# Two edits to a planned two-layer encoder kernel: output transposes due later, and the order of four low-rank products

## The chip, the cores and the metric

The kernel runs on one core of a Trainium2 chip, as one program. The metric is the device time of an execution in microseconds (us). A core has five engines with queues of their own: TensorE (PE in the rows; PEld is its weight loads), VectorE (DVE), ScalarE (ACT), GpSimd (POOL) and SyncE (SP, which only issues DMAs here).

## What is computed

Two layers. Each normalises its input, projects it once, sends the columns of the projection through four head groups, and maps the four gated outputs back.

```python
for l in range(DEPTH):                       # 2 layers, 1024 tokens, width 1024
    h = rms_norm(x, norm_pre[l])
    p = h @ w_in[l]                          # one projection, columns split among A, B, C, D
    y_a = head_layer_norm(mlstm(...) * sigmoid(a_o)) * silu(a_z)           # A: chunks of a matrix memory
    decay_logit = rwkv_w0[l] + jnp.tanh(w_lo) @ rwkv_w_up[l]               # B: low-rank up-projection 1
    a_b = sigmoid(rwkv_a0[l] + a_lo @ rwkv_a_up[l])                        # B: low-rank up-projection 2
    y_b = (head_layer_norm(rwkv7_scan(...)) + gn_b + bonus) * silu(b_z)    # B: delta rule
    y_c = rglru(...) * silu(c_z)                                           # C: gated linear recurrence
    y_d = head_layer_norm(retention(...)) * silu(d_z)                      # D: retention
    y = concat([y_a, y_b, y_c, y_d]) @ w_out[l]
    x = x + rms_norm(y, norm_post[l])
```

## The kernel before, in words

**Units.** Each head group is cut into four units of two heads (A0 to D3). A unit has projection pieces (products of the normalised input with weight columns, in PSUM banks of tag `pj`, three of them), and a mixer, a Python generator that handles the 1024 tokens in four quarters of 256. The mixers of A, D and C work in the two PSUM banks of tag `mx`, those of B in the three banks of tag `bc`.

**Order.** Nobody waits for anything while the program is written out: a planner (`Clock`, `Driver`) keeps a model of each engine's time and decides from it which step is written next into the queues. `Driver.run` (line 535) looks at five threads of mixer steps. A step may be written when its own time has come (the modelled end of its last step plus `SLACK`, 1.0 us) and two banks of its tag are free by the model. When no thread can go, a stretch of a projection piece is written instead: projections fill the gaps. On the chip TensorE takes its matmuls in the order so written, and waits where an operand or a bank is late.

**Output transposes.** A quarter of a mixer of A, D or B ends with a layer norm over each head (`ln_groups`, line 575: VectorE reductions, a square on ScalarE, a power on GpSimd, and as last step a VectorE multiply `t<-t,sm` or `bl<-bl,smB`). Its result has to be transposed. That is not written at once: `drv.later` (line 525) notes a closure, with the due time `clock.step + LATE`, where `clock.step` is the modelled end of the step that holds the norm. `Driver.run` writes the closure once it is due and one bank of its tag (`mx` for A and D, `bc` for B) is free by the model:

```python
self.flush(*[kind for kind, (t, _) in self.ends.items() if t <= now and clock.banks("bc" if kind == "B" else "mx", 1) <= now])
```

The next norm of the same kind writes it in any case (`drv.flush`, lines 1035, 1199, 1300). The closure is `out_a` (line 1207, for A and D) or `end` (line 1042, for B): a PSUM bank, two 128x128 transposes on TensorE, one ScalarE read of the bank, for B one VectorE add, and a store to DRAM by SP. There are 64 of `out_a` (4 quarters, 8 units, 2 layers) and 32 of `end`.

**Low-rank up-projections.** `prep` (line 812), a stage of B that runs 32 times, computes the two up-projections into two banks `wps` and `aps`. The weights are split in a high and a low part (`lu[0]`, `lu[1]`); for each bank there is one full product (128 rows: high weights times both parts of the input) and one half-row product (64 rows: low weights times the high part), the two accumulating in the bank. The half-row products of the two banks use rows 0 to 63 and rows 64 to 127. Behind them stand the two products of `head_sums` with a matrix of ones (`psbc<-cc,onesr` in the rows).

All instructions are recorded through one wrapper, so every row carries line 256; tiles tell them apart: `psmx<-ident,t` are the transposes of `out_a`, `psbc<-ident,bl` those of `end`, `psbc<-lora,luh` the full low-rank products, `psbc<-lora,lul` the half-row ones.

Of the kernel before, what the change touches and what calls it, by code (L numbers as in the profile page):

```python
# [132 lines left out]
TM = 2  # L133
NAT = [3,5,7,9]
CH = 6
SLACK, LATE = 1.0, 2.5
STEP = "step"
QA = 256
QB = 256
# [123 lines left out]
def trunk(ctx: ExitStack, tc, x, wch, wa, wd, wg, wo, pv, gb, lup, lrw, npost, cst, dtab, out):  # L263
    nc = tc.nc
    clock = Clock()
    V, A, Pl, PE, DQ = (Timed(e, n, clock) for e, n in ((nc.vector, "DVE"), (nc.scalar, "ACT"), (nc.gpsimd, "POOL"), (nc.tensor, "PE"),
                                                        (nc.sync, "SP")))
# [8 lines left out]
    def T(tag, shape, dt=F32):  # L276
        uid[0] += 1
        t = sb.tile(list(shape), dt, tag=tag, bufs=BUFS[tag], name=f"{tag}_{uid[0]}")
        if tag != "pr":
            clock.place(tag, clock.key(t), BUFS[tag])  # L280
        return t
# [16 lines left out]
    def PT(tag):  # L298
        uid[0] += 1
        t = psum.tile([128, 512], F32, tag=tag, bufs=PSB[tag], name=f"ps{tag}_{uid[0]}")  # L300
        clock.place("ps" + tag, clock.key(t), PSB[tag])
        return t
# [474 lines left out]
    def unit_b(l, P, hTs, j, drv):  # L777
# [34 lines left out]
        def prep(qt):  # L812
# [5 lines left out]
            lu = st["lu"]  # L818
# [6 lines left out]
            lo_ = T("lora", (128, 2, QB), F32R)  # L825
# [7 lines left out]
            wps = PT("bc")  # L833
            aps = PT("bc")
            for n, p in enumerate((wps, aps)):
                hp = slice(64 * n, 64 * n + 64)
                PE.matmul(p[:, 0:QB], lu[0][:, n, :], lo_[:, n, :], start=True, stop=False)
                PE.matmul(p[:, 0:QB], lu[1][hp], lo_[hp, n, :], start=False, stop=True)
            nps = PT("bc")
            head_sums(nps, kparts)  # L840
# [213 lines left out]
        def preps():  # L1054
            yield lambda: st["p"] == 6 and P.lora_done

            raw = bt((128, 2, 128))
            for n in range(2):
                for part in range(2):
                    DQ.dma_start(raw[64 * part:64 * part + 64, n, :], lup[l, 64 * n:64 * n + 64, j * 128:(j + 1) * 128])  # L1060
            lu = (T("luh", (128, 2, 128), F32R), T("lul", (128, 128), F32R))
            A.copy(lu[0], raw)
            for n in range(2):
                hp = slice(64 * n, 64 * n + 64)
                V.tensor_tensor(lu[1][hp], raw[hp, n, :], lu[0][hp, n, :].bitcast(F32), ALU.subtract)
            st["lu"] = lu
            for qt in range(S // QB):
                yield from prep(qt)
# [512 lines left out]
```

## Time and profile before

| | |
|---|---|
| median of 3 runs | 2573.94 us (2569.77 to 2581.92) |
| the profiled execution, its own time | 2583.34 us |
| span of the profiled execution, first to last instruction | 2581.6 us |
| TensorE matmuls, busy | 2407.5 us (93%), 16032 instructions |
| VectorE busy | 1788.8 us (69%) |
| ScalarE busy | 1036.4 us (40%) |
| GpSimd busy | 407.4 us (16%) |
| mean granted TensorE clock | 0.978 of full |

A row of the timeline gives the start, the time from the first start to the last end of the instructions it merges, the engine, the operation, out<-in by the program's names, shapes, and how many (x2). Brackets at its end give the idle time of the engine just before it and what ended that. Ends of matmuls are modelled, so the distance between two starts tells more about TensorE than a duration. A wait is charged to what came last: a transpose that waits "for DVE t" may wait for the norm's result or for a PSUM bank that a VectorE instruction was reading.

### The profile page before, as it was taken

Reading aid. Unit: us, or ns where it says so; the run is one execution under the profiler, and the core shown is the slowest. Engines: PE = TensorE matmul, PEld = TensorE weight load, DVE = VectorE, ACT = ScalarE, POOL = GpSimd, SP = SyncE. Lnnn points to the kernel's source line nnn. Section 1 sums busy time; section 2 is a strip of 40 time slices with the busy share of each in tenths; the row PEclk is TensorE's granted clock in tenths of the full one; section 3 lists DMA queues with packets and bytes.
Section 4 is the critical chain, followed back from the end, with each engine's and each line's share of the span. In section 5 each row is a group of like instructions: output and inputs, shape, how many; then the busy total and the mean of one; then the engine's idle time right before and its main releaser. Section 6 shows DMA issues by size and latency. Waiting matters only on the chain. (4 is left out here: it accounts for less than half of the span.)

```text
span 2581.6 us, 45006 instructions
## 1 busy us (share of the span) xinstructions
PE 2407.5 (93%) x16032; PEld 1977.6 (77%) x16032; DVE 1788.8 (69%) x5526; ACT 1036.4 (40%) x2261; POOL 407.4 (16%) x536
## 2 busy tenths in 40 slices
PE   7999999999999999999999989999999999999998
PEld 5787887787787777777777878877877877777776
DVE  5668877878767767455476678778787777763464
ACT  5323434534533543233354234336344335533333
POOL 2202212112111110001122111211121111100010
PEclk9999999999999999999999999999999999999999
DMA  5322232222323233275533222322223222333764
GB/s 157 106 61 75 63 88 81 72 74 77 89 74 79 67 106 102 86 245 186 187 121 104 59 74 69 88 79 64 73 82 90 68 77 81 95 98 118 249 205 150
DMA packets 219237, 265.82 MB, mean 103 GB/s; under 512 B 72708, under 2 KB 122244, under 8 KB 219012
## 3 DMA queue, kind: packets, MB, share of 16 engines
q1 hardware_dynamic: 210308, 254.54, 32.9%
q0 software_dynamic: 8704, 8.39, 1.4%
q8 instruction: 127, 2.08, 0.3%
q14 instruction: 98, 0.80, 0.1%
HBM read 201.76 MB, written 61.08 MB: 102 GB/s over the span
## 5 line engine op out<-in xcount | busy, mean ns | idle before, releaser
L256 PE MATMUL pspj<-hT,hi 128*128 128x512 f32 x2880 | 950.0, 409 | 3.6 <-ACT hT L256 2.7
L256 PEld LDWEIGHTS pspj<-hT,hi 128*128 128x128 f32 x2880 | 524.9, 192 | 107.8 <-ACT hT L256 3.2
L256 PE MATMUL pspj<-hT,lo 128*128 128x512 f32 x1440 | 573.6, 398 | 0.0
L256 PE MATMUL pspj<-hi,hT 128*128 128x256 f32 x2048 | 418.0, 294 | 0.3 <-ACT hi L256 0.3
L256 ACT CAST hi<-raw 128x512 fp32r<-128x512 f32 x372 | 229.7, 618 | 384.3 <-PE pspj L256 214.8
L256 PEld LDWEIGHTS pspj<-hi,hT 128*128 128x128 f32 x2048 | 337.8, 196 | 6.7 <-issue 1.3
L256 PEld LDWEIGHTS pspj<-hT,lo 128*128 128x128 f32 x1440 | 275.0, 191 | 59.4 <-DVE lo L256 0.4
L256 DVE TENSOR_TENSOR lo<-raw,hi 128x512 fp32r<-128x512 f32 x306 | 216.1, 707 | 146.5 <-ACT hi L256 142.8
L256 PE MATMUL pspj<-lo,hT 128*128 128x256 f32 x1024 | 294.9, 288 | 4.6 <-DVE lo L256 4.6
L256 PEld LDWEIGHTS pspj<-lo,hT 128*128 128x128 f32 x1024 | 200.6, 196 | 5.8 <-DVE lo L256 5.3
L256 DVE SCALAR_TENSOR_TENSOR NT<-PA,NT 128x20 f32<-128x20 f32 (+15 forms) x768 | 147.3, 243 | 68.7 <-DMA PA<-pd 64.4
L256 POOL TENSOR_TENSOR lo<-raw,hi 128x512 fp32r<-128x512 f32 x66 | 87.1, 1320 | 554.4 <-ACT hi L256 476.9
L256 POOL TENSOR_TENSOR sm<-sm,mhalf 128x4 f32<-128x4 f32 (+1 forms) x96 | 88.1, 918 | 455.0 <-DVE sm L256 361.1
L256 ACT ACTIVATE t<-t 128x256 f32<-128x256 f32 (+1 forms) x132 | 54.4, 412 | 215.0 <-DVE t L256 200.8
L256 PE MATMUL pspj<-hi,pr 128*128 128x512 f32 x384 | 132.6, 399 | 1.1 <-DVE c L256 1.1
L256 PE MATMUL psbc<-hi,pr 128*128 128x512 f32 x384 | 131.1, 395 | 0.0
L256 DVE SCALAR_TENSOR_TENSOR pr<-c,pv,pr 128x512 f32<-128x512 f32 x144 | 109.0, 757 | 10.7 <-ACT pr L256 9.7
L256 PE MATMUL psmx<-pr,t 128*128 128x65 f32 (+3 forms) x768 | 112.5, 282 | 1.9 <-DVE t L256 1.9
L256 POOL TENSOR_TENSOR cc<-bt,cc 128x256 fp32r<-128x256 f32 x64 | 51.2, 807 | 343.3 <-ACT cc L256 340.8
L256 PEld LDWEIGHTS psmx<-pr,t 128*128 128x128 f32 x768 | 101.8, 198 | 3.9 <-DVE t L256 2.6
L256 DVE TENSOR_TENSOR NT<-NT,inv 128x24 f32<-128x24 f32 (+13 forms) x480 | 94.9, 198 | 8.1
L256 DVE TENSOR_SCALAR bS<-psbc,wc 64x64 f32<-64x64 f32 x256 | 74.3, 290 | 37.3 <-PE psbc L256 31.1
(274 smaller groups left out, 4064.4 us busy)
## 6 DMA issues: line engine op xcount, KB each, us to landing
raw<-in_wch_dram SPq DMA_DIRECT2D x180, 256.0 KB
raw<-in_wo_dram SPq DMA_DIRECT2D x128, 256.0 KB
PA<-pd SPq DMA_DIRECT2D x64, 256.0 KB
zmix<-c SPq DMA_DIRECT2D x64, 256.0 KB
rkv<-ymix SPq DMA_DIRECT2D x64, 256.0 KB
rkv<-c SPq DMA_DIRECT2D x48, 256.0 KB
rkv<-rkv SPq DMA_DIRECT2D x32, 384.0 KB
lora<-lora POOLq DMA_DIRECT2D x32, 256.0 KB, 3.5
```

The costliest lines, as they stand in the source:

```text
L256: res = fn(*args, **kw)
```

## The change

`LATE` goes from 2.5 to 6.0 us: the transposes of a norm become due 3.5 us of modelled time later. In `prep` the two full products come first, then the two half-row ones. The planner sees both, and may write everything behind them in another order. No instruction is added or taken away.

```diff
@@ -133,7 +133,7 @@
-SLACK, LATE = 1.0, 2.5
+SLACK, LATE = 1.0, 6.0
@@ -833,8 +833,9 @@
             for n, p in enumerate((wps, aps)):
+                PE.matmul(p[:, 0:QB], lu[0][:, n, :], lo_[:, n, :], start=True, stop=False)
+            for n, p in enumerate((wps, aps)):
                 hp = slice(64 * n, 64 * n + 64)
-                PE.matmul(p[:, 0:QB], lu[0][:, n, :], lo_[:, n, :], start=True, stop=False)
                 PE.matmul(p[:, 0:QB], lu[1][hp], lo_[hp, n, :], start=False, stop=True)
```

## Rows read from the trace of the kernel before

**Rows 1.** The page, part 1: busy time of each engine, share, instructions.
```profile
PE 2407.5 (93%) x16032; PEld 1977.6 (77%) x16032; DVE 1788.8 (69%) x5526; ACT 1036.4 (40%) x2261; POOL 407.4 (16%) x536
```

**Rows 2.** Waits of PE: who, for whom, us in total, times, longest.
```profile
PE psmx L256 <- DVE t L256: 49.3, 36, 3.5
```

**Rows 3.** Groups of PE: busy us, mean ns | idle us before, releasers.
```profile
L256 PE MATMUL psmx<-ident,t 128*128 128x128 f32 x128 | 26.8, 292 | 38.6 <-DVE t L256 35.9 <-DVE inv L256 2.4
...
L256 PE MATMUL psbc<-ident,bl 128*128 128x128 f32 x64 | 12.8, 282 | 3.7 <-DVE NT L256 1.2 <-DVE bl L256 1.0 <-ACT bt L256 1.0
```

**Rows 4.** Timeline of PE: transposes that waited, and steps behind two of them.
```profile
216.04 0.44 PE L256 MATMUL psmx<-ident,t 128*128 128x128 f32 x2 [1.15 <-DVE t L256]
...
385.54 0.44 PE L256 MATMUL psmx<-ident,t 128*128 128x128 f32 x2 [2.63 <-DVE t L256]
...
389.12 0.58 PE L256 MATMUL psmx<-aS,t 128*128 128x130 f32 x1
...
593.61 0.44 PE L256 MATMUL psmx<-ident,t 128*128 128x128 f32 x2 [2.33 <-DVE t L256]
...
594.97 0.65 PE L256 MATMUL psmx<-aS,t 128*128 128x130 f32 x2 [0.22 <-issue]
...
806.15 0.44 PE L256 MATMUL psmx<-ident,t 128*128 128x128 f32 x2 [3.45 <-DVE t L256]
```

**Rows 5.** Timeline of DVE around three of these waits.
```profile
215.55 0.43 DVE L256 TENSOR_TENSOR t<-t,sm 128x256 f32<-128x256 f32 x1 [0.82 <-POOL sm L256]
...
380.88 0.42 DVE L256 TENSOR_TENSOR t<-t,sm 128x256 f32<-128x256 f32 x1 [0.35 <-POOL sm L256]
...
385.06 0.42 DVE L256 SCALAR_TENSOR_TENSOR t<-psmx,t 128x256 f32<-128x256 f32 x1
...
385.47 0.42 DVE L256 SCALAR_TENSOR_TENSOR t<-psmx,t 128x256 f32<-128x256 f32 x1
...
594.44 0.42 DVE L256 TENSOR_TENSOR t<-pr,t 128x256 f32<-128x256 f32 x1
```

**Rows 6.** Windows at half clock behind eight waits: busy us, PEclk, DMA, GB/s.
```profile
386.89:390.30 3.41, 3.41 (x29) 2.96 (x27) 2.62 (x9) 1.62 (x4) 1.46 (x2) 0.50 0.39 118
...
806.73:816.97 10.24, 10.20 (x42) 7.85 (x41) 5.94 (x17) 3.54 (x10) 0.00 (x0) 0.50 0.13 27
...
sum 47.80, PE 47.71 PEld 38.52 DVE 28.27 ACT 16.99 POOL 3.17; mean PE 5.96 PEld 4.81 DVE 3.53 ACT 2.12 POOL 0.40
```

**Rows 7.** Timeline of PE: one of the 32 low-rank groups, and its neighbours.
```profile
204.31 0.28 PE L256 MATMUL pspj<-hi,hT 128*128 128x256 f32 x1
204.43 0.28 PE L256 MATMUL psbc<-lora,luh 128*128 128x256 f32 x1
204.64 0.38 PE L256 MATMUL psbc<-lora,lul 64*128 64x256 f32 x1
204.95 0.38 PE L256 MATMUL psbc<-lora,luh 128*128 128x256 f32 x1
205.27 0.38 PE L256 MATMUL psbc<-lora,lul 64*128 64x256 f32 x1
205.58 0.50 PE L256 MATMUL psbc<-cc,onesr 128*128 128x256 f32 x2
```

**Rows 8.** Timeline of PE: half-row products that alternate between the two row halves.
```profile
225.22 0.38 PE L256 MATMUL psbc<-ident,KB 128*128 128x128 f32 x2
225.53 1.16 PE L256 MATMUL psbc<-AR,KB 64*128 64x128 f32 x16
226.62 0.38 PE L256 MATMUL psmx<-aS,t 128*128 128x130 f32 x1
```

**Rows 9.** Timeline of PE: last transposes of B in layer 1, first output product.
```profile
1095.02 0.38 PE L256 MATMUL psbc<-ident,bl 128*128 128x128 f32 x2
...
1103.43 0.39 PE L256 MATMUL psmx<-hi,pr 128*128 128x512 f32 x1
```

**Rows 10.** Waits of SP's queue: stores of transposed outputs among them.
```profile
SPq L256 <- ACT t L256: 139.5, 35, 11.9
```

## The prediction

> **What bounds the kernel.** I read the engines' busy shares first. TensorE is busy for 2407.5 of 2581.6 us and the next engine, VectorE, for 69% [rows 1]: the end is set by TensorE's queue, so what counts is its idle time (174 us), its pace, and its switches. The second view is who TensorE waited for: the largest entry is 49.3 us in `mx` banks for VectorE's `t` [rows 2]. Grouped by instruction, most of it stands in front of the output transposes of A and D: 38.6 us, and 3.7 us in front of B's [rows 3]. The timeline shows 25 waits of over 0.4 us there (38.3 us, 1.53 us each), 13 in the first layer and 12 in the second; the other 39 pairs hardly wait.
>
> What they wait for is the point. Some wait for the norm: at 216.04 the pair starts as the norm's multiply ends (215.55 + 0.43) [rows 4, 5]. These are about 9.6 us. The rest (about 29 us) wait for a bank. At 385.54 the norm's multiply had ended at 381.30, but VectorE's read of a score bank ended at 385.48, and that is when the pair started [rows 4, 5]: the planner held the bank for free and the chip was later than the model. The third view is the granted clock: behind eight of these waits it fell to half (0.50, the 1.2 GHz level) for 47.8 us in all; TensorE was busy in 47.71 of them [rows 6]. At half the pace that is up to 23.9 us of lost work.
>
> **Part 1, the later due time.** Nothing is added; what moves is, 64 times, two transposes, a ScalarE read and an SP store, and 32 times the same with a VectorE add. Ends of the gain: nothing, and 38.6 + 3.7 + 23.9 = 66.2 us.
>
> The norm kind should vanish: no transpose of that kind is later than its place by more than 1.97 us, and the move is 3.5. For the bank kind the question is what is late next. I walked behind each of the 25 waits to the next step whose operand was fresh. Three classes:
> - Free: the pair at 385.54 waited 2.63 us. The next step of that chain is at 389.12, and its last score operand was ready at 385.89 [rows 4, 5]. Moved up by 2.63 it would start at 386.5 and not wait. Six waits are like this, 11.1 us; I count 10.
> - Taken over: the pair at 593.61 waited 2.33 us, but the recurrence step at 594.97 starts 0.1 us after its own operand (594.44 + 0.42) [rows 4, 5]. Without the transposes TensorE comes to that step earlier and waits there. Nine waits, 12.2 us; I count nothing, and leave their half clock too.
> - Between: ten waits, 14.9 us, the two longest (3.45 us at 806.15 [rows 4], and its twin in the second layer) among them; another transpose wants the next `mx` bank behind them. I count a third, 5 us.
>
> So 15 of 38.3 us. The clock by the same classes: of the 47.8 us at half, 6.8 lie behind free waits (386.89 to 390.30 is one), 17.1 behind taken-over ones, 23.9 behind those between (10.24 at 806.73, its twin the same, 3.4 elsewhere) [rows 6]. Half of a stretch is lost work: 3.4 us come back in the first class and half of 12 in the third: 9.4 us. B's 3.7 us I leave.
>
> What the move can cost: the pairs now come among the recurrence steps, which take `mx` banks too, and a bank that the model calls free can be held there as well. No row shows those places. The nearest row is the present place [rows 3]: 25 of 64 waiting, 1.53 us each. The ends are none waiting (nothing) and all 64 (98 us). I take four, 6 us, nearer to none, because the 39 pairs that do not wait already arrive later behind their norm than the waiting ones. The store moves with its transposes: SP waited 139.5 us for ScalarE's `t` [rows 10], with loads behind; a store that is written later lets the loads written meanwhile pass. I count that as nothing: no wait of TensorE in the mixers is ended by a DMA or by SP. B's transposes are the last of the layer's mixers at 1095.02, and the projections fill TensorE until 1103.43 [rows 9]: 8.4 us cover a later B; beyond that each us costs one. After the last step of all, the closure is written at once in either kernel.
>
> Part 1: 15 + 9.4 - 6 = 18 us gained.
>
> **Part 2, the four products.** Starts before: full 204.43, half-row 204.64, full 204.95, half-row 205.27, ones 205.58 [rows 7]: 1.15 us from the first to the next work. A 256-column product behind one of the same shape takes 0.12 us (204.31 to 204.43), so nearly all the rest is switching: 0.21 us into half rows from a streaming full product, 0.31 us from half to full rows, and 0.32 again. After: full to full 0.12, full to half 0.21, half to half, half to ones 0.31. The two half-row products lie in different row halves and banks. Of such a mix there is a row: sixteen products of 128 columns in alternating halves take 226.62 - 225.53 - 0.31 = 0.78 us, 0.052 each, while full-row ones of 128 columns are 0.11 apart (0.38 less the 0.27 of one) [rows 8]. So two go in the time of one, and the second adds about 0.01 here. Sum: 0.65 us, a gain of 0.50 us, times 32 = 15.9 us. Ends: if the pair does not run side by side (0.12) and the entry costs 0.31, it is 0.86 us and a gain of 0.29 us, 9.3 us in all. I take 0.50, the row of the same mix of halves. TensorE stands at no operand there, so it is on the path; but where the next wait hangs on older work of another engine it is eaten. Some 170 waits in 2582 us are one per 15 us; with operand chains of some 3 us that is one group in five: 12.7 us.
>
> Read by durations the result would be another: the half-row product is shown with 0.38 us and the full one with 0.28 [rows 7]. The Trainium skill, Perfetto Trace Analysis, section on per-instruction lifecycle, says that a matmul's end is estimated from its size and not observed; the starts here agree, being 0.12 us apart under bars of 0.28. By durations alone the edit would bring nothing, since all four bars stay. The Trainium skill, TensorEngine Tiling (Array Packing), Key Properties, says that changing the tiling mode drains the array and that tiles of one mode run in parallel; the rows of the switches and of the alternating halves agree, and by that rule alone the whole 0.50 us holds.
>
> **Sum.** 18 + 13 = 31 us, 1.2%. From the profiled execution: 2583 - 31 = 2552. That one is 9.4 us above the median of the three, so the median goes to 2574 - 31 = 2543.
>
> **Rivals.**
> - Carried over: every wait moves to the next step of the chain, or the due time does not decide because the bank condition does. For: nine waits are of that kind already. Against: six are not. Part 1 is then 0 - 6, part 2 gives 13: 2567, within half a per cent. Chance 0.22.
> - All of it: no wait is left and the clock stays up: 66 + 16 = 82 us, 2492; between it and the forecast lie the times around 2510. For: 3.5 us exceeds all 25 waits. Against: the taken-over class. Chance 0.12.
> - Slower: the transposes collide with the recurrence in the two `mx` banks. Place: the pair between two state steps, whose bank VectorE empties late. Price: 1.53 us a wait plus 0.95 us of clock (23.9 / 38.6 of it), 2.48 us. It uses up part 2 when 5 more pairs wait than now (30 of 64), and makes the kernel slower by over half a per cent from 35. With all 64: 97 us lost against 13, 2658. For: rows at 385 and 806 show the model early by up to 3.5 us. Against: the late readers there stood behind DMAs that have landed by the new place. Chance 0.14.
> - My forecast, part of the waits and most of part 2: 0.52, with a range of its own of 2522 to 2560.
>
> **How the numbers follow.** Half a per cent, 13 us, is about what a measurement of this kernel can tell from no change. Faster by more: nearly all of the forecast (0.50), the all-of-it case (0.12), a fifth of the carried-over one (0.05): 0.67. Slower by more: most of the collision case, 0.12. Same: 0.21. The range runs from 2508, half-way into the all-of-it case, to 2582, past the carried-over one and the start of the collision.
>
> **What would show it.** Right: idle before `psmx<-ident,t` falls from 38.6 to some 10 us; idle before `psmx<-aS,t` and `psmx<-pr,t` grows by less than 15; the stretch at half clock near 806 gets shorter or goes; the starts from the first `luh` to `onesr` are 0.65 us apart, the two `lul` within 0.02. Wrong: idle in front of the transposes stays and its releaser is `aS` or `dS`; or the recurrence steps wait for ScalarE's `t<-psmx`; or a gap opens between B's last transposes and the output product; or the planner, whose whole order shifts with both edits, puts new waits in places that no row here shows.

## The result, and the profile after

The changed kernel takes 2596.7 us (median of 4 runs, 2590.1 to 2598.6) against 2574.5 of the kernel before in the same job: a ratio of 1.0075, 95% interval 1.0046 to 1.0103. It is 22 us slower by the medians (19 by the ratio); the forecast was 31 us faster. The profiled execution has a span of 2593.9 us, 12.3 above that of before, and it is this pair that the rows below compare.

First what the edits were meant to do. The page's first part, against [rows 1]:

```profile
PE 2385.5 (92%) x16032; PEld 1973.8 (76%) x16032; DVE 1779.6 (69%) x5526; ACT 1030.5 (40%) x2261; POOL 414.3 (16%) x536
```

TensorE is busy for 22 us less with the same instructions; the low-rank groups below account for 15.4 of them. Groups of TensorE (busy us, mean ns, idle us before and its releasers), first after:

```profile
L256 PE MATMUL psmx<-hi,pr 128*128 128x512 f32 x256 | 93.0, 405 | 16.8 <-ACT pr L256 16.1 <-ACT hi L256 0.8
...
L256 PE MATMUL psmx<-pr,pr 64*128 64x128 f32 x256 | 37.3, 317 | 32.4 <-DVE t L256 24.6 <-ACT pr L256 6.0 <-DVE inv L256 1.4
L256 PE MATMUL psmx<-ident,t 128*128 128x128 f32 x128 | 26.3, 288 | 10.9 <-DVE t L256 6.4 <-ACT cc L256 4.6
L256 PE MATMUL psmx<-aS,t 128*128 128x130 f32 x112 | 24.4, 300 | 13.5 <-issue 11.4 <-DVE t L256 1.3 <-DVE aS L256 0.9
...
L256 PE MATMUL psbc<-ident,bl 128*128 128x128 f32 x64 | 12.9, 284 | 13.9 <-DVE bl L256 13.9
```

and three of the same groups before (the other two are in [rows 3]):

```profile
L256 PE MATMUL psmx<-hi,pr 128*128 128x512 f32 x256 | 91.4, 397 | 3.0 <-ACT pr L256 2.0 <-ACT hi L256 0.9
...
L256 PE MATMUL psmx<-pr,pr 64*128 64x128 f32 x256 | 33.3, 303 | 12.5 <-DVE t L256 7.9 <-DVE NT L256 3.1 <-DVE inv L256 1.4
...
L256 PE MATMUL psmx<-aS,t 128*128 128x130 f32 x112 | 25.9, 315 | 2.7 <-issue 1.8 <-DVE aS L256 0.8
```

Idle time in front of the output transposes fell from 38.6 us [rows 3] to 10.9, as forecast. Part of it came back: 32.4 us in front of `psmx<-pr,pr` (12.5 before) and 13.5 in front of `psmx<-aS,t` (2.7 before), 31 us more in two groups; and 16.8 us stand in front of the output products (`psmx<-hi,pr`, 3.0 before) and 13.9 in front of B's transposes (3.7 before). By release, TensorE's waits in `mx` banks for `t` went from 49.3 [rows 2] to 35.5 us; `psmx` for ScalarE's `pr` and `psbc` for `bl` are the new ones:

```profile
PE psmx L256 <- DVE t L256: 35.5, 30, 3.3
PE psbc L256 <- DVE bS L256: 25.1, 26, 2.1
PE psmx L256 <- ACT pr L256: 23.3, 7, 7.2
PE psbc L256 <- DVE TQ L256: 16.8, 12, 3.0
PE psbc L256 <- DVE bl L256: 13.9, 4, 5.4
```

SP's queue, with the later stores in it, hardly changed (139.5 us in [rows 10]):

```profile
SPq L256 <- ACT t L256: 145.9, 41, 17.9
```

The low-rank group does what was forecast. Timeline of TensorE (start, us, ..., idle before in brackets):

```profile
1480.07 0.40 PE L256 MATMUL psbc<-lora,luh 128*128 128x256 f32 x2
1480.39 0.38 PE L256 MATMUL psbc<-lora,lul 64*128 64x256 f32 x2
1480.70 0.50 PE L256 MATMUL psbc<-cc,onesr 128*128 128x256 f32 x2
```

From the first `luh` to `onesr` 0.63 us, where 0.65 were forecast and 1.15 were read before [rows 7]; the two half-row products end 0.38 us after the first of them starts, which is the length of one. Summed over the 32 groups this distance fell from 41.2 to 25.8 us, by 15.4.

TensorE thus has less to do, and the projections of a layer end earlier: the last one of layer 1 ends at 1087.96, in the kernel before at 1103.6. Its waits only moved: from a layer's first low-rank product to its last projection TensorE stands idle for 65.8 and 70.2 us in the two layers, against 63.4 and 65.6 before. And the layer does not end earlier. Timeline of TensorE at the end of layer 1, against [rows 9]:

```profile
1093.40 0.58 PE L256 MATMUL psbc<-bS,TQ 128*128 128x128 f32 x2 [0.70 <-DVE bS L256]
1099.37 0.66 PE L256 MATMUL psbc<-ident,bl 128*128 128x128 f32 x2 [5.38 <-DVE bl L256]
1106.82 0.80 PE L256 MATMUL psmx<-hi,pr 128*128 128x512 f32 x1 [6.78 <-ACT pr L256]
```

and of layer 2:

```profile
2386.05 0.66 PE L256 MATMUL psbc<-ident,bl 128*128 128x128 f32 x2 [5.39 <-DVE bl L256]
2393.96 0.79 PE L256 MATMUL psmx<-hi,pr 128*128 128x512 f32 x1 [7.25 <-ACT pr L256]
```

B's last transposes moved from 1095.02 to 1099.37 in layer 1 (in layer 2 from 2374.36 to 2386.05), and nothing is left to lie over them: TensorE waits 5.4 us for B's last norm, then 6.8 us until the stored result has been loaded again, together with its gate, and made an operand. Windows of 10 us there (busy us of PE, PEld, DVE, ACT, POOL, then the granted clock):

```profile
1080.00:1090.00 10.00, 9.78 (x108) 7.30 (x107) 2.75 (x7) 4.13 (x10) 1.68 (x3) 1.00 0.16 54
1090.00:1100.00 10.00, 2.54 (x10) 1.34 (x10) 4.60 (x17) 1.14 (x3) 1.01 (x1) 0.68 0.18 53
1100.00:1110.00 10.00, 3.22 (x9) 2.47 (x9) 3.19 (x5) 1.80 (x3) 0.00 (x0) 0.50 0.73 225
```

In the kernel before the same three windows are full:

```profile
1080.00:1090.00 10.00, 10.00 (x48) 8.28 (x47) 4.83 (x12) 2.85 (x7) 0.00 (x0) 1.00 0.31 107
1090.00:1100.00 10.00, 10.00 (x46) 8.25 (x45) 4.05 (x8) 2.80 (x6) 1.36 (x1) 1.00 0.46 146
1100.00:1110.00 10.00, 10.00 (x44) 7.91 (x43) 5.70 (x10) 4.01 (x7) 1.28 (x1) 1.00 0.88 290
```

In all, from a layer's first low-rank product to its first output product, layer 1 grew by 2.6 us (1012.8 to 1015.4) and layer 2 by 9.5 (1014.6 to 1024.1): 12.1 of the 12.3 us.

So a layer has two limits: TensorE's queue with its filler (the projections that are written into the gaps), which got shorter, and B's sixteen quarters, which got longer. **B's chain** is read below as the time from the start of the layer's first `psbc<-lora,luh` to the start of its last `psbc<-ident,bl`: 1004.4 and 1005.9 us before, 1008.0 and 1016.2 after. Two quarters of B are in flight; the first stage of a quarter is written only when the mixer of the quarter two before it is done (`drv.mixed`).

### The profile page after: what moved, and what is told of

Same layout as the page of the kernel before. It is cut to its first block, busy times and chain, and to the rows that moved or that the text cites. A ratio compares the mean times of both kernels' runs of the same rounds, so it can differ in the third digit from the quotient of the medians.

```text
span 2593.9 us, 45063 instructions
## 1 busy us (share of the span) xinstructions
PE 2385.5 (92%) x16032; PEld 1973.8 (76%) x16032; DVE 1779.6 (69%) x5526; ACT 1030.5 (40%) x2261; POOL 414.3 (16%) x536
## 5 line engine op out<-in xcount | busy, mean ns | idle before, releaser
L256 PE MATMUL pspj<-hT,hi 128*128 128x512 f32 x2880 | 946.7, 408 | 2.7 <-ACT hT L256 2.3
L256 PEld LDWEIGHTS pspj<-hT,hi 128*128 128x128 f32 x2880 | 525.8, 192 | 109.1 <-issue 3.6
L256 PE MATMUL pspj<-hT,lo 128*128 128x512 f32 x1440 | 574.2, 399 | 0.0
L256 PE MATMUL pspj<-hi,hT 128*128 128x256 f32 x2048 | 417.9, 294 | 0.8 <-ACT hi L256 0.8
L256 ACT CAST hi<-raw 128x512 fp32r<-128x512 f32 x372 | 229.5, 619 | 387.4 <-PE pspj L256 205.5
L256 PEld LDWEIGHTS pspj<-hi,hT 128*128 128x128 f32 x2048 | 339.3, 197 | 5.9 <-ACT hi L256 1.2
L256 PEld LDWEIGHTS pspj<-hT,lo 128*128 128x128 f32 x1440 | 275.5, 191 | 60.4
L256 DVE TENSOR_TENSOR lo<-raw,hi 128x512 fp32r<-128x512 f32 x306 | 212.9, 699 | 154.2 <-ACT hi L256 152.7
L256 PE MATMUL pspj<-lo,hT 128*128 128x256 f32 x1024 | 296.1, 289 | 3.7 <-DVE lo L256 3.7
L256 DVE SCALAR_TENSOR_TENSOR NT<-PA,NT 128x16 f32<-128x16 f32 (+15 forms) x768 | 150.4, 246 | 89.8 <-DMA PA<-pd 85.2
L256 PEld LDWEIGHTS pspj<-lo,hT 128*128 128x128 f32 x1024 | 201.7, 197 | 4.6 <-DVE lo L256 4.1
L256 POOL TENSOR_TENSOR lo<-raw,hi 128x512 fp32r<-128x512 f32 x66 | 90.7, 1376 | 629.4 <-ACT hi L256 505.1
L256 POOL TENSOR_TENSOR sm<-sm,mhalf 128x4 f32<-128x4 f32 (+1 forms) x96 | 90.4, 941 | 447.1 <-DVE sm L256 411.8
L256 PE MATMUL pspj<-hi,pr 128*128 128x512 f32 x384 | 132.7, 399 | 0.0
L256 PE MATMUL psbc<-hi,pr 128*128 128x512 f32 x384 | 130.9, 394 | 0.0
L256 ACT ACTIVATE t<-t 128x256 f32<-128x256 f32 (+1 forms) x132 | 54.1, 411 | 187.2 <-DVE t L256 176.7
L256 DVE SCALAR_TENSOR_TENSOR pr<-c,pv,pr 128x512 f32<-128x512 f32 x144 | 108.5, 753 | 7.0 <-ACT pr L256 6.3
L256 PE MATMUL psmx<-pr,t 128*128 128x65 f32 (+3 forms) x768 | 108.4, 277 | 0.3 <-DVE t L256 0.3
L256 PE MATMUL psmx<-hi,pr 128*128 128x512 f32 x256 | 93.0, 405 | 16.8 <-ACT pr L256 16.1
L256 POOL TENSOR_TENSOR cc<-bt,cc 128x256 fp32r<-128x256 f32 x64 | 52.6, 829 | 347.9 <-ACT cc L256 326.1
L256 DVE TENSOR_TENSOR NT<-NT,inv 128x24 f32<-128x24 f32 (+13 forms) x480 | 95.9, 200 | 8.7
L256 PEld LDWEIGHTS psmx<-pr,t 128*128 128x128 f32 x768 | 97.6, 193 | 2.3 <-DVE t L256 0.8
```

The lines of the kernel that those rows point to most:

```text
L256: res = fn(*args, **kw)
```

## The experiments

Eighteen kernels beside the two; each ratio is to the runs of the kernel before in the same job, with its 95% interval. "Plan" is what the planner's own model gives for the place of B's last quarter, in us from the start of layer 1; the last two columns are B's chain as defined above, each from one profiled execution. Executions of the same kernel differ (2570.8 to 2592.1 us for the kernel before in one job), so differences of a few us in these columns mean little.

```
run                     median   ratio (interval)          plan  B's chain, layer 1, 2
before                  2574-79  1                         1012  1004.4  1005.9
after                   2596.7   1.0075 (1.0046-1.0103)    1039  1008.0  1016.2
e1_late_only            2605.6   1.0112 (1.0083-1.0141)    1039  1013.9  1011.8
e2_order_only           2597.5   1.0087 (1.0060-1.0113)    1014  1004.4  1016.0
e3_late_a_only          2607.7   1.0124 (1.0099-1.0149)    1036  1021.0  1014.8
e4_late_b_only          2605.9   1.0104 (1.0075-1.0133)    1029  1015.1  1017.7
e5_after_held           2595.2   1.0066 (1.0042-1.0091)    1017  1015.7  1009.9
e6_late_held            2547.0   0.9881 (0.9860-0.9902)     997   981.9   986.4
e7_order_held           2595.4   1.0074 (1.0044-1.0103)    1016  1010.3  1005.9
e8_after_more_filler    2604.4   1.0106 (1.0069-1.0142)       -  1018.9  1004.4
e9_before_lean          2572.9   0.9982 (0.9963-1.0001)    1010   997.2   998.1
e10_before_late_1_5     2596.8   1.0068 (1.0048-1.0088)    1043  1009.9  1014.9
e11_order_late_5        2547.8   0.9880 (0.9859-0.9902)    1001   985.7   981.2
e12_both_held_late_5    2576.2   0.9980 (0.9960-1.0000)     999  1003.2   996.5
e13_old_list_products   2569.1   0.9964 (0.9946-0.9981)       -   995.8  1001.9
e14_old_list_both       2572.1   0.9966 (0.9949-0.9984)       -   997.2   993.9
e15_new_list_undone     2614.5   1.0142 (1.0114-1.0169)       -  1017.1  1031.5
e16_late5_list_undone   2577.0   0.9999 (0.9982-1.0017)       -   996.0   990.8
e17_new_list_c_moved    2606.2   1.0101 (1.0077-1.0125)       -  1016.0  1024.0
e18_old_list_c_moved    2580.0   1.0000 (0.9985-1.0015)       -  1001.3  1004.3
```

### Which edit is it? e1 to e4

e1 has `LATE` 6.0 with the old order of the products, e2 the new order with `LATE` 2.5. e3 and e4 have both edits, with `LATE` 6.0 for one kind of transposes alone:

```diff
-            self.ends[kind] = clock.step + LATE, fn
+            self.ends[kind] = clock.step + (LATE if kind == "A" else 2.5), fn     # e3; e4: "B"
```

> The due time alone (6.0 us; the four products in the old order). Cover theory: what sets a layer's end is B's chain of quarters, and projections are only filler; a shorter filler moves no end once B's last transposes and the 7.5 us from there to the first output product are bare. The late due time then makes B's last transposes later and is the edit that costs: 8 to 22 us slower than before, a gap of 5 us or more in front of the first output product in each layer. Collision theory: the loss is new waits of TensorE inside the mixers; 10 to 30 us slower with no gap at the layer's end.

> The four products alone (due time 2.5 us as before). Both theories: starts of the group 0.65 us apart instead of 1.15, so 8 us less filler a layer. Cover theory: the first output product can begin at the earliest 7.5 us behind B's last transposes, it began 8.4 us behind, so at most 1 us a layer comes out, plus or minus what the planner's new order moves B's last transposes: within 6 us of before. TensorE theory (all that TensorE is spared comes out): 12 to 16 us faster.

> Both edits, but the due time of 6.0 us only for A's and D's transposes; B's are due after 2.5 us as before. If B's own late transposes lengthen B's chain, this one has B's last transposes where they were and is within 6 us of before, or faster by up to 4. If A's and D's late transposes delay B (they hold nothing of B's, but shift the planner's order), it is as slow as the changed kernel, 10 to 22 us.

> Both edits, but the due time of 6.0 us only for B's transposes. If B's own late transposes lengthen the chain: 10 us or more slower, as the changed kernel. If it is A's and D's: within 6 us of before.

The expectations do not decide it: e1 is 29 us slower, with TensorE bare at the layer's end, where the cover theory had at most 22; e2 fits neither theory; e3 and e4, meant to tell the two kinds of transposes apart, are both as slow as the changed kernel or slower (1.0124 and 1.0104). Each edit alone is slower, by 1.1 and 0.9%, and both together are no slower than one. That effects don't add up like this speaks against costs of the edits themselves; what all five kernels share is that the planner wrote a new order. e13 to e16 test it.

### A stay in B's chain, and a hold against it: e5 to e7

In the changed kernel quarter 5 of B (counted from 0) stands in layer 1 for 24.5 us between the start of its last inverse products and its first product with the state; in before no quarter stays over 6.1 us there. Timeline of TensorE, after:

```profile
474.93 0.67 PE L256 MATMUL psbc<-G,AP 64*64 64x128 f32 x16
...
495.86 0.40 PE L256 MATMUL psmx<-TQ,lrl 128*128 128x512 f32 x1
...
499.39 0.49 PE L256 MATMUL psbc<-bS,TQ 128*128 128x128 f32 x2 [1.77 <-DVE TQ L256]
```

VectorE ran the inversion of the other quarter from 466.8 to 487. The hold lets an inversion be written only while B's other quarter is not between these two steps:

```diff
-            yield lambda: st["ready"] >= qt
+            yield lambda: st["ready"] >= qt and not drv.tq     # set ahead of the TQ step, cleared behind it
```

e5 is the changed kernel with the hold, e6 is e1 with it, e7 is e2 with it.

> The changed kernel, but an inversion is not written while B's mixer stands between its AP products and the VectorE step that makes TQ. Collision with the inversion (new theory): in the changed kernel the planner writes the inversion of one quarter of B (a run of small VectorE steps some 20 us long) just ahead of the TQ step of the other, so the first state product follows the G,AP products after 24.5 and 16.3 us in two quarters of layer 1, where before it was never over 6.1. Held back, no quarter is over 9 us, the first output product comes 15 us or more a layer earlier, and the kernel is 14 to 36 us faster than the changed one: 2560 to 2583. Mixer-waits theory (bank waits of TensorE in the mixers cost the time): the hold touches no mx bank, so within 6 us of the changed kernel, 2590 to 2603.

> The late due time alone with the same hold. New theory: its two or three long gaps a layer (27.3, 23.9 and 14.5 us in layer 1) go, 57 us of gaps a layer, and with them 20 us or more: 2560 to 2585, and under that of the late due time alone (2605) in any case. Mixer-waits theory: 2598 to 2612.

> The new order of the products alone with the same hold. New theory: its gaps of 9.2 and 10.8 us go, some 20 us a layer; B's last transposes then come 5 to 10 us earlier in layer 2, and the kernel is within 8 us of before, or faster: 2564 to 2586. If gaps of 10 us have nothing to do with it, it stays at 2597.

In e5 the longest stay is 12.9 us, and the time is that of the changed kernel: the stay that the theory blamed does not explain it. e6 gained 58 us over e1, more than the theory had, e7 nothing over e2. e1 and e6 issue the same instructions; the order alone is worth 2.3%.

### Does TensorE's work set the time? e8, e9

e8 adds a projection piece per layer to the changed kernel, with a result that nobody reads (22 us of TensorE in all). e9 takes TensorE work away from the kernel before:

```diff
-                    for a, b in ((hi, 0), (hi, 1), (lo, 0)):
+                    for a, b in ((hi, 0), (hi, 1), (lo, 0))[:terms]:     # terms = 1 for C2 and C3 gates
```

> The changed kernel with one more projection piece at the end of each layer's pieces, whose result is thrown away: 48 products of 0.23 us, 11 us of TensorE a layer. Chain theory (B's chain of quarters sets the layer's end, TensorE's end is bare for some 19 us): within 5 us of the changed kernel. TensorE theory (its work sets the end): 22 us more than the changed kernel.

> The kernel before with its old order of steps, but the last two gate projections of each layer (C2 and C3) take one of their three partial products (high times high) and leave the other two out: 64 products of 512 columns fewer a layer, 0.23 us each, 14.7 us of TensorE work a layer, 29.5 us in all, all of it behind the last decisions that matter to B, so that the planned places of B's quarters stay as they are (1010 us from the layer's start in the plan, against 1012). Theory 'B's chain of quarters sets the end of a layer, and projections only fill': the projections then end some 6 us before B's last transposes, TensorE stands bare behind these, and the time falls by 1 us a layer at most, within 4 us of before (2575 to 2580 where before has 2579). Rival 'TensorE's queue sets the end', on which the forecast was built: 29 us faster, 2550; half way, 2564, would mean that both bind.

e8 costs 8 of its 22 us (1.0106 against 1.0075); with the two intervals that is anything from -4 to 20 us, so it tells little. e9 spares 29.5 us and gains 6.0 (2572.9 against 2578.8, interval of the ratio from no gain to 9.5 us). Timeline of TensorE at the end of its layer 1:

```profile
1079.71 3.92 PE L256 MATMUL pspj<-hT,hi 128*128 128x512 f32 x16
...
1088.17 0.66 PE L256 MATMUL psbc<-ident,bl 128*128 128x128 f32 x2 [4.54 <-DVE bl L256]
...
1095.48 0.79 PE L256 MATMUL psmx<-hi,pr 128*128 128x512 f32 x1 [6.65 <-ACT pr L256]
```

The last projection ends at 1083.6 and TensorE stands bare behind B, as in the changed kernel. This run breaks the premise of the forecast: of the 29.5 us that TensorE is spared in the last fillers of a layer, at most a third reaches the end of the program. (Work spared inside B's own stages is another matter: e13 below.)

### Does the plan foretell it? e10 to e12

e10 changes `LATE` from 2.5 to 1.5 and nothing else, e11 is the changed kernel with `LATE` 5.0, e12 is e11 with the hold.

> The kernel before with LATE 1.5 instead of 2.5 and nothing else. The planner's own plan of it has B's last quarter written 1043 us after the start of the first layer (before: 1012). Theory 'the plan's length of B's chain carries over to the chip': slower by about as much as the other plans of that length, 2595 to 2612. Rival 'what counts is the waits in front of the transposes': they wait a little more than before, up to 64 pairs by 1 us less what they already wait, most of it hidden: 2575 to 2590.

> The changed kernel with LATE 5.0 instead of 6.0: both edits are there, the transposes still come 2.5 us later than before, and the four products are in the new order. Its plan has B's last quarter at 1001 us and the layer's end at 1025 (changed kernel: 1039 and 1044). Theory 'the plan's length of B's chain decides': B's chain on the chip is about 985 to 995 us a layer instead of 1008 to 1016, and the time 2545 to 2570, faster than before. Rival 'the edits themselves cost': as the changed kernel or the order alone, 2590 to 2600. A result at 2595 with B's chain at 1010 would say that the plan's figure does not carry over.

> Both edits with LATE 5.0, and the hold on the inversion of the other quarter while B's mixer stands between its A P products and its TQ step. Plan: B's last quarter at 999 us, end at 1023, the shortest among plans with the new order of the products. Theory 'the plan's length of B's chain decides': as the held kernel with the old order (2547), perhaps less by what the low-rank groups give inside B's chain (0.5 us, 16 times a layer): 2535 to 2560. Rival 'the new order of the products costs in itself, as the two runs that have it alone (2597 and 2595) suggest': 2590.

Two hits and a miss. e10, with less delay instead of more, is as slow as the changed kernel. e11 has both edits and is 1.2% faster than before; from the changed kernel it differs by 1.0 us of modelled time. Its groups and the end of its layer 1 (timeline of TensorE):

```profile
L256 PE MATMUL psmx<-ident,t 128*128 128x128 f32 x128 | 25.2, 278 | 10.1 <-DVE t L256 10.0
...
L256 PE MATMUL psbc<-ident,bl 128*128 128x128 f32 x64 | 13.5, 295 | 2.8 <-ACT bt L256 2.7
```

```profile
1076.51 0.38 PE L256 MATMUL psbc<-ident,bl 128*128 128x128 f32 x2
...
1089.00 0.39 PE L256 MATMUL psmx<-hi,pr 128*128 128x512 f32 x1
```

The wait in front of the transposes is that of the changed kernel (10.1 against 10.9), so it cannot make the difference of 49 us; B's last transposes are at 1076.51 instead of 1099.37, and 12.5 us of projections cover what follows. e12 misses: its plan is as short as e11's, its chain is 18 and 15 us longer. Over the 20 kernels the time goes with B's measured chain (sum of both layers; correlation 0.96, 0.85 us for each us), and with the plan's figure only roughly: e2, e7 and e12 are off by 1%. A correlation is not yet a cause, and the chain is not always what ends a layer. In e6, e11, e12 and e16 the projections end last, 12.5 to 15.2 us behind B's last transposes; e16 has a chain 23.5 us shorter than before over both layers (both from profiled executions) and the same time.

### Edits and order taken apart: e13 to e16

The planner's decisions were recorded (about 1050 a layer: which thread's step, which projection stretch, which transposes come next) and written out as a fixed list. With the list of before and no edit the finished program has the order of before, line by line.

```diff
-        def run(self):
-            while True:
+        def run(self, order):
+            first = list(self.threads)
+            for c in order:
...
-                for th in self.threads:
+                    th = first[int(c)]          # "p": a projection stretch, "A", "B", "D": transposes
```

> The planner's decisions of the kernel before, recorded and replayed as a fixed list (which step, which projection stretch, which transposes come next), with only the four products of the low-rank group in the new order; LATE plays no part. Theory 'the order written by the planner decides, the edit itself is harmless': B's quarters gain 0.5 us each in their first stage, eight of them in a row in a layer's chain, so 0 to 8 us faster than before: ratio 0.997 to 1.000. Rival 'the new order of the products costs in itself' (the runs with it alone gave 2597 and 2595): ratio 1.006 to 1.009. Rival 'TensorE's queue sets the end', the forecast: 12.7 us faster, 0.995.

> The replayed list of the kernel before, with both edits: the new order of the products, and the transposes written where the rule with LATE 6.0 puts them along that list. Theory 'the order written by the planner decides': within 12 us of before, on the faster side rather: ratio 0.995 to 1.002. Rival 'the edits cost in themselves': as the changed kernel, 1.006 to 1.010. The forecast's sum (31 us from TensorE's queue) would be 0.988.

> The replayed list of the changed kernel with both edits undone: the products in the old order, the transposes where the rule with LATE 2.5 puts them along that list. Theory 'the order written by the planner decides': slow like the changed kernel, whose list it follows, ratio 1.004 to 1.012, with the two long stays of a quarter of B per layer in front of its first state product. Rival 'the edits cost in themselves': back at before, 0.997 to 1.002.

> The replayed list of the fast kernel with both edits and LATE 5.0 (2548 us), with both edits undone as in the run before this one. Theory 'the order written by the planner decides': fast like the kernel whose list it follows, with a few us more for the products and the waits in front of the transposes: ratio 0.988 to 0.994. Rival 'LATE 5.0 and the products bring the gain themselves': 0.997 to 1.002.

As a table (ratio to before):

```
list written for     edits undone   edits made
kernel before        1              0.9966  (products alone 0.9964)
LATE 6.0 (changed)   1.0142         1.0075
LATE 5.0             0.9999         0.9880
```

In each of the three lists the edits gain: 0.34%, 0.67% and 1.19%, 9 to 31 us. What makes the changed kernel slow is its list: with the edits undone it is 1.42% slower than before, a loss of 36 us, of which the edits give 17 back. The ends of the lists show what became of the cover. Each list has 490 projection stretches (`p`) a layer; that of before ends in `00ppppppBpppppp`, that of `LATE` 5.0 in `00ppppppppBppppppppp`, and that of the changed kernel in `0pp0pp0-0-0-0-00B`: its stretches are used up ahead of B's last steps (`0`; `B` stands for its transposes, `-` for idle time of TensorE in the plan). Beside the transposes and the four products, 1 to 2% of TensorE's products stand a few places off in e14 and e15. The expectation for e16 failed: the fast list is worth nothing without the edits, and the pair is worth 1.2%, so list and edits don't simply add. In e14 the idle time in front of the transposes fell to 11.6 us as in the changed kernel, yet e13, without that, is as fast:

```profile
L278 PE MATMUL psmx<-pr,pr 64*128 64x128 f32 x256 | 35.4, 308 | 16.1 <-DVE t L278 13.8 <-DVE inv L278 2.1
L278 PE MATMUL psmx<-ident,t 128*128 128x128 f32 x128 | 26.8, 289 | 11.6 <-DVE t L278 11.3
```

(groups of TensorE in e14; `L278` is the same wrapper as `L256`). In that list the later transposes bring nothing that can be measured beside the new order of the products (0.9966 against 0.9964, to within about 6 us).

### What in the list? e17, e18

All 38 stays of over 11 us in the traces up to e16 have gate products of unit C (`psmx<-TQ,lrl`, as in the rows at 495.86) in them; without these no stay is over 10.1 us. B and C share the one buffer `TQ`, so B's step waits for C's products. e17 moves C's steps out of that place in the slow list (`4` is a step of C, `0` one of B's mixer, `1` an inversion), e18 moves one into it in the list of before:

```diff
-...p03p03p2144p033pp3pAp3pp3pp4p0...      # e17, quarter 5; the 0s: A P step, TQ step, first state step
+...p03p03p21p04433pp3pAp3pp3pp4p0...
-...p30p4440Appp21p03p04p...               # e18, quarter 5
+...p30p0Appp21p4403p404p...
```

> The replayed list of the changed kernel with both edits in, but with three steps of unit C a layer moved by a few places: the weights and the first split of C0, and the second split of C1, stand in the slow list between B's A P step and its TQ step (quarters 5 and 8), and now stand just behind that TQ step. So B takes the one TQ buffer before C does, and needs no longer wait for C's gate products. Theory 'the shared TQ buffer makes B's chain longer': the two long stays a layer (24.5 and 16.3 us) fall to under 10 us, the two quarters of the chain that followed from them get 10 to 16 us shorter each, and the time falls by 25 to 55 us: 2540 to 2572, against 2597. Rival 'the stays are slack, and other work fills what they give back', as the held inversion suggested: 2588 to 2600.

> The converse: the replayed list of the kernel before, no edit, but with three steps of C0 moved by a few places: weights, first split and first gate products stand in it just ahead of B's A P step of quarter 5; now the weights and the split stand just ahead of its TQ step and the gate products behind it. Theory 'the shared TQ buffer makes B's chain longer': quarter 5 of each layer stays over 15 us (4 before) between its last inverse product and its first state product, B's last transposes come some 8 to 16 us later a layer, and the time rises by 12 to 35 us: 2590 to 2613, against 2578. Rival 'such a stay is slack': within 8 us of before.

Neither came as the theory said. e17 is no faster than the changed kernel (1.0101 against 1.0075). The second stay (quarter 8, 16.3 us) went, but the next first stage of B stands where the list has it, 21.1 us behind the last state product (11.0 in the changed kernel). At the first one (19.4 us instead of 24.5) `TQ` is now ready early, and B waits all the same:

```profile
478.15 0.67 PE L278 MATMUL psbc<-G,AP 64*64 64x128 f32 x16
...
497.54 0.38 PE L278 MATMUL psbc<-bS,TQ 128*128 128x128 f32 x2
```

```profile
483.58 0.27 DVE L278 TENSOR_TENSOR TQ<-cst_sb,psbc 128x128 f32<-128x128 f32 x1
```

```profile
484.00:497.50 13.50, 11.79 (x60) 9.70 (x61) 11.88 (x43) 4.75 (x9) 0.00 (x0) 1.00 0.23 60
```

```profile
L278 PE MATMUL pspj<-hT,hi 128*128 128x512 f32 x28 | 9.1, 404 | 0.0
L278 PE MATMUL pspj<-hT,lo 128*128 128x512 f32 x14 | 5.5, 394 | 0.0
```

(timelines of TensorE and VectorE, the window between them, and TensorE's largest groups in it.) The last part of `TQ` is written at 483.58; the state product starts at 497.54, without a wait of TensorE: 42 projection products stand ahead of it in the queue. The list holds B back by where it puts B's step among the filler, not only by the buffer. In e18 the stay became 9.9 us in layer 1 and 10.8 in layer 2 instead of over 15, and the time did not move, so it tests the theory only in part. That the shared buffer makes the slow list slow is therefore not shown. That each long stay has C's products in it is an observation; which of the planner's decisions is at fault stays open.

## Why the prediction was wrong, point by point

- **"The end is set by TensorE's queue."** This step failed, and the sum stood on it. A busy share of 93% says that TensorE is the engine with the most work, not that a layer ends when it runs out of work. In the kernel before the projections do end last (1103.6), but B's chain lies close under them: where TensorE is bare, the first output product follows B's last transposes by some 7.5 us (1106.82 - 1099.37; e9: 1095.48 - 1088.17), and 8.41 stood there before. After about 1 us a layer the chain sets the end. e9 shows the price: 29.5 us of TensorE in the last fillers are worth 6. The Trainium skill, Perfetto Trace Analysis, sections Identifying the Most-Contended Engine and Optimization Strategy, says to find that engine by occupancy and to optimize it first, through the gaps between its slices. The gaps were found, and closing them was worth little here (e14 against e13): the measurement decides against that reading for this kernel, whose busiest engine is filled with work that can be moved.
- **"8.4 us cover a later B", costed at nothing.** The rows were right [rows 9], their reading was not. The cover has to hold those 7.5 us from B's last transposes to an operand, so 1 us of it was free. And the gain that was forecast is taken out of the cover itself: projections that end 15.6 us earlier lie over nothing at the end. The text had named this gap among the things that would prove it wrong, but no term of the sum had it.
- **Part 1, 15 us out of the waits and 9.4 out of the clock.** Two of the signs came true: the idle time in front of the transposes fell to 10.9 us ("some 10"), and that in front of `psmx<-aS,t` and `psmx<-pr,t` together grew by 9 (under 15). The sum failed all the same. TensorE's idle time up to the last projections did not fall by the 9 us of the sum (15 less 6), it rose from 129.0 to 136.0 in the two layers; 20 us of it stand in front of `psmx<-pr,pr` (12.5 to 32.4), which neither the sum nor the signs named. Outside the two bare layer ends the time at half clock fell from 114.6 to 106.4 us, about 4 us of work, though the stretch near 806 did shrink from 10.2 to 3.4. On the old list (e14 against e13) part 1 is worth nothing, to within about 6 us, where 18 us were forecast.
- **Part 2.** Right in mechanism and size at its place, 0.52 us in the group shown and 15.4 in all (15.9 in the sum); 12.7 us were forecast, e13 gives 9 (interval 5 to 14). The fifth taken off for eaten gains is within that interval. The Trainium skill, TensorEngine Tiling (Array Packing), Key Properties, says that a change of the tiling mode drains the array and that tiles of one mode run in parallel; the groups agree (two switches fewer and the pair side by side, 0.52 us), which the bars of the four products, nearly as long as before, don't show.
- **"The planner, whose whole order shifts".** Named as what could go wrong, with no price and no chance. It decided the sign: 36 us. The variants show what it would have needed: re-planned orders of nearly the same instructions lie between 0.988 and 1.012, so a change that this planner sees has a term of about one per cent either way. The plan could have been read ahead of the forecast, since it comes out as the program is written: B's last quarter at 1039 us where the kernel before has 1012. It is a rough guide (e5 has 1017 and is as slow), but it pointed to slower.
- **The rivals.** "Slower by collisions in the `mx` banks" has the right sign and another mechanism: waits at the transposes did not grow. "Carried over" describes the waits inside the mixers best (129.0 to 136.0 us).
- **A number that meets by luck.** e11 is 31 us faster, the very figure of the forecast, but not by its mechanism: against e16, the same list with the edits undone, TensorE's idle time from a layer's first low-rank product to its first output product rose from 124.0 to 139.4 us, and its busy time fell by 40 us.

With the table of the lists the result reads: 36 us lost by the list, 17 gained by the edits; by ratios 1.42% - 0.67% = 0.75%. Taken in the other order it is 9 gained by the edits on the old list, 22 less than forecast, and 28 lost by the new one (1.0075 against 0.9966).

## What to carry to other kernels

Where a planner writes the order, an edit has two effects: its own, which a replay of the old order with the edit made shows (here 9 us gained), and that of the new order, which may be larger and of either sign (here 36 us lost); neighbouring values of a parameter sample the second (`LATE` 5.0 gives 2547.8 us, 6.0 gives 2596.7, 1.5 gives 2596.8). Ahead of a forecast, name for each stage which chain ends last and what covers it, and take the forecast's own savings out of that cover; and read the new plan. A long stay in a trace is not yet a cost: take it out with the rest of the order held fixed.

## What the runs showed of the hardware

- Products that use one half of the rows each start together, 2 to 5 ns apart in all 32 low-rank groups of the changed kernel, where 0.62 us lay between them before: the second half-row product adds nothing to the 0.31 us from the first one to the next full-row work (1480.39 to 1480.70), in two row halves and two banks.
- Where TensorE stands bare at a layer's end, its granted clock falls to 0.50, the 1.2 GHz level: 17.07 us in layer 1 of the changed kernel, from 1093.67, with 4.90 us of work in them, and 17.1 us in layer 2. The first output products run at half pace behind it (0.80 us for the first 512-column one, where it is 0.39 in the kernel before). So each bare end of this kernel costs twice, in the wait (5.4 and 6.8 us) and in the work at half pace, by estimate half of the 4.90 us:

```profile
1093.67:1110.74 17.07, 4.90 (x13) 3.42 (x13) 6.18 (x14) 2.94 (x6) 1.01 (x1) 0.50 0.46 143
```
